# Both parts of the activations as one moving operand in the feature-major products of a two-block network

## The chip, the cores and the metric

One NeuronCore of one Trainium2 chip runs the whole kernel; inputs and outputs lie in the chip's memory. The metric is the device time of one execution in microseconds (us). Engines are named as in the profile: PE is TensorE's matmul, PEld its weight load, DVE is VectorE, ACT is ScalarE, POOL is GpSimd and SP is SyncE, which issues the DMAs of the weights.

## The reference

256 tokens of 2048 features (T = 256, D = 2048) go through two network blocks in float32. Nearly all arithmetic is products of the activations with weight matrices.

```python
def first_block(x, ...):                       # block 1
    h = rms_norm(x, norm1_w)
    proj = h @ w_in                            # 2048 x 10792
    q, kv, gates, dn_qkv, z, a, b, merge_g = split(proj)
    nsa = nsa_mixer(...) @ w_up_nsa            # attention, 1024 x 2048
    dn  = gated_deltanet(...) @ w_up_dn        # delta rule, 1024 x 2048
    x = x + (sigmoid(merge_g[0]) * nsa + sigmoid(merge_g[1]) * dn) @ w_o
    h = rms_norm(x, norm2_w)
    x = x + (silu(h @ w_ffn_gate) * (h @ w_ffn_up)) @ w_ffn_down   # 2048 x 5632, twice; 5632 x 2048
...
# block 2: RWKV-7 heads and latent attention (MLA) side by side, @ w_out, then
#   silu(causal_conv(h @ ffn_w_gate)) * (h @ ffn_w_up), @ ffn_w_down, closing norm
```

## The kernel before

A float32 matrix is written as a sum of two float32r parts, hi and lo. A product keeps three of the four part products: hi times hi, hi times lo, lo times hi (`mm3`, L288 to L292). Each weight tile is loaded raw (`wraw`, 512 KB), cast to hi by ACT (L259), and the rest is formed as lo by DVE (L260); the emission of the two is moved ahead of other work (`high_priority`). There are 5 raw, 3 hi and 3 lo buffers. `wchunks` (L265) loads 1024 // n rows of 128 at a time where a product is n < 512 columns wide, and two rows where n is 512.

Two kinds of product exist. Token-major (`gemm_tok`, L294): the activations are stationary and 512 weight columns move. Feature-major (`gemm_feat`, L304): a 128 x 128 block of the weights is stationary and the 256 tokens move; four blocks m = 0 to 3 (nm = 4; in `Rwkv.project` two) fill one tile `mmA` of PSUM, [128, 4, 256], over the kt = 16 (in `merge_up` 8) rows k of the weights. One block of one row is three matmuls of 256 columns. Of the pool `psA` there are two such tiles, two banks each; the other four banks are `pB`.

The two parts of the activations H lie in two 16 KB areas (slots b and c, or d and e; `hh` and `hl` in block 2's feed-forward). The results leave PSUM in one DVE or ACT operation of up to 1024 columns, mostly together with the multiplication by the norm's row scale (`rb`). Feature-major are: `Nsa.first` and `Nsa.q`, `DeltaNet.project` (its results wait in the list `raw`, at most two, for `conv`), `merge_gate`, `merge_up`, gate and up of both feed-forwards, and `Rwkv.project` (out by `padded`). By hand, and not through `gemm_feat`, are `Nsa.kv` (L1083), `Rwkv.small`, `small_proj` and `Mla.project` (L1716); the last has moving operands in two runs of 128 columns (L1739, L1740).

In the mixers of both blocks several chains of steps are emitted side by side by `weave`, which estimates when a step is ready; a product yields a filler step per row k. `K.later` holds the turning of a finished piece of x into H (`turn`: PE transposes, ACT makes hi, DVE lo); it is emitted after the fourth row of the next product.

Of the kernel before, what the change touches and what calls it, by code (L numbers as in the profile page):

```python
# [37 lines left out]
def make_consts():  # L38
    """shape-only tables: identity, triangular masks, block masks, rotary tables of the first block"""
# [82 lines left out]
class Traced:  # L122
    """an engine of nc whose calls are also counted"""
# [82 lines left out]

class Kern:
    def __init__(self, tc, A, out, ctx):
# [43 lines left out]
    def wsplit(self, raw, view, n):  # L252
        """raw tile [P, 1024], n elements used -> float32r (hi, lo) views with hi + lo == raw"""
# [11 lines left out]
    def wchunks(self, W, kt, c0, n, wk0=0, cols=None):  # L265
        """yields (k, hi, lo): the k-th 128 rows of W[:, c0:c0+n], or of the column ranges `cols`"""
# [21 lines left out]
    def mm3(self, o, a, b, start, stop):  # L288
        """o += (a0 + a1).T @ (b0 + b1) less the product of the two low parts"""
# [4 lines left out]
    def gemm_tok(self, X, W, kt, c0, n, xk0=0, wk0=0):  # L294
        """[tokens, n columns] in PSUM [P, 2, 512]; X = (hi, lo) [P, kt, T]; a step per 128 rows of W"""
# [8 lines left out]
    def gemm_feat(self, X, W, kt, c0, nm=4, xk0=0, wk0=0):  # L304
        """[128 columns, tokens] blocks in PSUM [P, 4, T]; a step per 128 rows of W"""
        ps = self.psA.tile([P, 4, T], F32, name="mmA")
        for k, wh, wl in self.wchunks(W, kt, c0, nm * P, wk0):
            for m in range(nm):
                ms = slice(m * P, (m + 1) * P)
                self.mm3(ps[:, m, :], (wh[:, ms], wl[:, ms]), [a[:, xk0 + k, :] for a in X],  # L310
                         k == 0 and m % 2 == 0, k == kt - 1)
            yield FILL
        return ps

    def split(self, src, hi, lo, scale=None):
        """hi + lo = src * scale in float32r parts"""
# [20 lines left out]
    def square(self, out, x, t):  # L337
        """out = sum of the squares of the rows of x, [P, up to 512]"""
# [19 lines left out]
    def row_scale(self, st, n=D, out=None):  # L358
        """1 / rms of the rows"""
# [6 lines left out]
    def spread(self, r):  # L366
        """the rows' scales [P, 2] along the free dimension of every partition"""
# [7 lines left out]
    def rows(self, x, r):  # L375
        """x [P, 2, n] times r"""
# [24 lines left out]
    def wake(self):  # L401
        """while nothing has arrived: the clock of TensorE goes up, ScalarE gets a table"""
# [25 lines left out]
        # blocks of 8: every partition (row of the inverse) gets all of its block  # L428
# [15 lines left out]
        # pairs of blocks of b: minus (odd block of X) (L between them) (even block of X); the odd rows are kept together  # L444
# [38 lines left out]
def run(gen):  # L483
    """emit all the steps of a generator; its value"""
# [7 lines left out]
def together(*gens):  # L492
    """steps of several generators in turn; (generator, steps at a time) or one step each"""
# [28 lines left out]
class Cat:  # L522
    """the blocks of two tiles in a row"""
# [11 lines left out]
def hT_tiles(K, slots):  # L535
    return tuple(K.slot(s, [P, KD, T], F32R) for s in slots)


def hidden(K, pool, slots):
    """the inner activations of a feed-forward layer, (hi, lo)"""  # L540
    return tuple(Cat(K.slot(s, [P, KD, T], F32R), pool.tile([P, KF - KD, T], F32R, name="hid" + n)) for s, n in zip(slots, "hl"))


def block1(K, ctx):
    """the first block; every norm's row scale is applied to what is made of the rows, so that no product waits for it"""
# [4 lines left out]
    H = hT_tiles(K, "bc")  # L550
# [3 lines left out]
    def begin():  # L554
        """x by column groups, between the weights of the first projection"""
# [17 lines left out]
    with ExitStack() as mix:  # L573
# [33 lines left out]
    H = hT_tiles(K, "de")  # L607
    run(add_proj(K, x, M, A["w_o"][0], KD, scale=0.5, after=norm_after(K, x, st, "norm2_w", H)))
    r = K.row_scale(st)
    with tc.tile_pool(name="ffn", bufs=1) as fp:  # L610
        hid = hidden(K, fp, "bc")
        for g in range(KF // 4):
            pg = run(K.gemm_feat(H, A["w_ffn_gate"][0], KD, 512 * g))
            if g == 0:
                rb = K.spread(r)
            sg = fp.tile([P, 4, T], F32, name="sg", bufs=2)
            rows4 = rb[:, None, :].to_broadcast([P, 4, T])
# [5 lines left out]
            K.split(sg, hid[0][:, 4 * g:4 * g + 4], hid[1][:, 4 * g:4 * g + 4])  # L623
        # x times the weight of the closing norm, with the sums for that norm and for the next
# [4 lines left out]
        H = hT_tiles(K, "de")  # L629
# [14 lines left out]
def norm_after(K, x, st, wname, H):  # L644
    """for add_proj: the pieces of x transposed and times the next norm's weight, and the sums of their squares"""
# [16 lines left out]
def add_proj(K, x, X, W, kt, scale=1.0, base=None, after=None, widths=(512,) * 4, **kw):  # L662
    """x += scale * (tokens of X) @ W, or x = x * base + that; `after` sees each piece"""
# [60 lines left out]
class DeltaNet:  # L724
# [1094 lines left out]
```

## Time and profile before

| | |
|---|---|
| time, median of 3 runs | 2887.51 us (2883.43 to 2891.77) |
| span of the profiled execution | 2890.4 us |
| PE busy | 2856.1 us, 99% of the span |
| DVE busy / ACT busy / POOL busy | 60% / 44% / 7% |
| weights and the rest read | 476.23 MB, 167 GB/s over the span |

The profiled execution has no other time than its span, from the first instruction to the last; it lies 2.9 us above the median and inside the range of the runs. In the rows, a PE matmul is listed with a duration longer than the distance from one to the next, since matmuls overlap in the array; distances are read from the starts, or from counts in a stretch in which PE is never idle.

### The profile page before, as it was taken

The numbers are of one execution on the slowest core, as the hardware profiler recorded it, in microseconds if no ns is written. First come the engines' busy times: TensorE is split into PE (matmuls) and PEld (weight loads), VectorE is DVE, ScalarE is ACT, GpSimd is POOL, SyncE is SP. The second block draws the span as 40 slices with busy tenths as digits, with TensorE's granted clock in tenths as the row PEclk, the third lists the DMA queues.
The fourth block names the chain that finished last, engine by engine and source line by source line (L and its number), as shares of the span: only waits on it lengthen the run. The fifth ranks groups of instructions, "written<-read, shape, count | busy, mean of one in ns | idle before, by whom it ended". The sixth has DMA issues, their size and how long they took to land.

```text
span 2890.4 us, 49301 instructions
## 1 busy us (share of the span) xinstructions
PE 2856.1 (99%) x20536; PEld 2654.7 (92%) x20536; DVE 1731.7 (60%) x2333; ACT 1270.6 (44%) x1568; POOL 204.3 (7%) x203
## 2 busy tenths in 40 slices
PE   9999999999999999999999999999999999999998
PEld 8997899999899999998888988888899999999888
DVE  6678557845555555554555685676575656655453
ACT  5447345434444444444444543444354444343443
POOL 0000000001000000000000221210000000000000
PEclk9999999999999999999999999999999999999999
DMA  7653256546666666666666652323466666666664
GB/s 233 205 153 106 84 167 178 162 129 189 215 182 184 183 181 188 182 183 188 198 196 195 189 146 74 99 73 115 142 172 190 183 182 183 183 183 189 193 193 139
DMA packets 285569, 484.68 MB, mean 168 GB/s; under 512 B 26113, under 2 KB 77057, under 8 KB 284706
## 3 DMA queue, kind: packets, MB, share of 16 engines
q1 hardware_dynamic: 282688, 475.88, 56.0%
q10 hardware_dynamic: 2658, 5.66, 0.6%
q8 instruction: 161, 2.64, 0.4%
q14 instruction: 62, 0.51, 0.0%
HBM read 476.23 MB, written 5.24 MB: 167 GB/s over the span
## 4 chain that ended last, share of the span: by engine, by line
PE 94%; DVE 3%; issue 1%; POOL 1%; ACT 1%; DMA 0%; ACTq 0%; DVEq 0%; POOLq 0%
PE mmA L134 83%; PE pB L134 11%; DVE wlo L260 1%; DVE MM L134 0%; DVE xn L134 0%; POOL psb L134 0%; DMA wA<-in_rwkv_w_dram 0%; DVE iw L134 0%; DVE sd L134 0%; DMA dn_nrm<-in_dn_norm_w_dram 0%; ACT whi L259 0%; POOL sa L134 0%; POOL xn L134 0%; DVE rt L134 0%; DVE Dm L134 0%
## 5 line engine op out<-in xcount | busy, mean ns | idle before, releaser
L260 DVE TENSOR_TENSOR wlo<-wraw,whi 128x1024 fp32r<-128x1024 f32 x889 | 1100.1, 1239 | 872.9 <-ACT whi L259 871.6
L259 ACT CAST whi<-wraw 128x1024 fp32r<-128x1024 f32 x889 | 928.2, 1045 | 1315.5 <-PE mmA L134 1250.3
L134 PE MATMUL mmA<-sd,whi 128*128 128x256 f32 x2256 | 604.7, 286 | 0.4 <-DVE xn L134 0.4
L134 PE MATMUL mmA<-sd,wlo 128*128 128x256 f32 x2048 | 582.2, 284 | 2.6 <-DVE wlo L260 2.6
L134 PE MATMUL mmA<-se,whi 128*128 128x256 f32 x2096 | 568.1, 284 | 1.2 <-DVE se L134 1.2
L134 PEld LDWEIGHTS mmA<-sd,whi 128*128 128x128 f32 x2256 | 420.6, 193 | 3.3 <-issue 1.6
L134 PE MATMUL mmA<-hh,whi 128*128 128x256 f32 x1408 | 398.7, 283 | 0.0
L134 PE MATMUL mmA<-hh,wlo 128*128 128x256 f32 x1408 | 398.5, 283 | 0.0
L134 PE MATMUL mmA<-hl,whi 128*128 128x256 f32 x1408 | 398.5, 283 | 0.0
L134 PEld LDWEIGHTS mmA<-sd,wlo 128*128 128x128 f32 x2048 | 394.6, 193 | 3.5 <-DVE wlo L260 3.0
L134 PEld LDWEIGHTS mmA<-se,whi 128*128 128x128 f32 x2096 | 393.1, 192 | 2.2 <-DVE se L134 1.4
L134 PE MATMUL mmA<-sb,whi 128*128 128x256 f32 x1152 | 332.7, 289 | 1.5 <-ACT whi L259 1.5
L134 PE MATMUL mmA<-sb,wlo 128*128 128x256 f32 x1152 | 329.3, 286 | 1.9 <-DVE wlo L260 1.9
L134 PE MATMUL mmA<-sc,whi 128*128 128x256 f32 x1152 | 328.8, 285 | 0.0
L134 PEld LDWEIGHTS mmA<-hl,whi 128*128 128x128 f32 x1408 | 270.3, 192 | 0.0
L134 PEld LDWEIGHTS mmA<-hh,whi 128*128 128x128 f32 x1408 | 270.3, 192 | 0.0
L134 PEld LDWEIGHTS mmA<-hh,wlo 128*128 128x128 f32 x1408 | 270.3, 192 | 0.0
L134 PEld LDWEIGHTS mmA<-sb,whi 128*128 128x128 f32 x1152 | 222.6, 193 | 3.9 <-ACT whi L259 1.7
L134 PEld LDWEIGHTS mmA<-sb,wlo 128*128 128x128 f32 x1152 | 222.7, 193 | 3.0 <-DVE wlo L260 2.3
L134 PEld LDWEIGHTS mmA<-sc,whi 128*128 128x128 f32 x1152 | 222.5, 193 | 1.4 <-issue 0.7
L134 PE MATMUL mmA<-whi,hidh 128*128 128x512 f32 (+1 forms) x504 | 184.2, 365 | 0.0
L134 PE MATMUL mmA<-wlo,hidh 128*128 128x512 f32 (+1 forms) x504 | 184.2, 365 | 0.0
(422 smaller groups left out, 3815.0 us busy)
## 6 DMA issues: line engine op xcount, KB each, us to landing
wraw<-in_w_in_dram SPq DMA_DIRECT2D x232, 512.0 KB, 3.7
wraw<-in_w_ffn_gate_dram SPq DMA_DIRECT2D x88, 512.0 KB, 3.9
wraw<-in_w_ffn_up_dram SPq DMA_DIRECT2D x88, 512.0 KB, 3.7
wraw<-in_w_ffn_down_dram SPq DMA_DIRECT2D x88, 512.0 KB, 4.5
wraw<-in_ffn_w_gate_dram SPq DMA_DIRECT2D x88, 512.0 KB, 3.8
wraw<-in_ffn_w_up_dram SPq DMA_DIRECT2D x88, 512.0 KB, 3.7
wraw<-in_ffn_w_down_dram SPq DMA_DIRECT2D x88, 512.0 KB, 3.7
wraw<-in_w_o_dram SPq DMA_DIRECT2D x32, 512.0 KB, 4.6
```

The lines of the kernel that those rows point to most:

```text
L134: r = f(out, *a, **k)
L259: nc.nc.scalar.copy(h, r)
L260: nc.nc.vector.tensor_sub(l, r, h.bitcast(F32))
```

## The change

`gemm_feat` computes two blocks (nm = 2) into the same PSUM tile, now [128, 2, 2, 256]. For each block the hi weights are stationary once and hi and lo of the activations move as one operand of 512 columns, in two runs of 256; then the lo weights are stationary and hi of the activations moves. So the first half of a block's bank holds hi·hi + lo·hi, the second half hi·lo. `fold` adds the halves: ACT copies the second half to SBUF, DVE adds the first half to it. H's two parts become one tile (`Parts`) so that one access covers both. Callers loop over groups of two blocks instead of four; the row scale is multiplied in SBUF after the fold; the list `raw` of the delta rule holds pairs of heads. The pool of the slots d and e is opened anew twice (`new_side`). `small_proj`, `Nsa.kv`, `Rwkv.small` and `Mla.project` stay as they are. The rest of the diff removes comments.

```diff
+class Parts:
+    def __init__(self, both):
+        self.both = both
+    def __getitem__(self, i):
+        return self.both[:, i]
+    def wide(self, k):
+        return self.both[:, :, k]
...
-    def gemm_feat(self, X, W, kt, c0, nm=4, xk0=0, wk0=0):
-        ps = self.psA.tile([P, 4, T], F32, name="mmA")
+    def gemm_feat(self, X, W, kt, c0, nm=2, xk0=0, wk0=0):
+        ps = self.psA.tile([P, 2, 2, T], F32, name="mmA")
         for k, wh, wl in self.wchunks(W, kt, c0, nm * P, wk0):
-            for m in range(nm):
-                ms = slice(m * P, (m + 1) * P)
-                self.mm3(ps[:, m, :], (wh[:, ms], wl[:, ms]), [a[:, xk0 + k, :] for a in X],
-                         k == 0 and m % 2 == 0, k == kt - 1)
+            self.wide(ps, X, xk0 + k, wh, wl, range(nm), k == 0, k == kt - 1)
             yield FILL
         return ps
+    def wide(self, ps, X, k, wh, wl, blocks, start, stop):
+        for m in blocks:
+            ms = slice(m * P, (m + 1) * P)
+            self.mm(ps[:, m], wh[:, ms], X.wide(k), start, stop)
+            self.mm(ps[:, m, 0], wl[:, ms], X[0][:, k], False, stop)
+    def fold(self, out, ps):
+        self.nc.scalar.copy(out, ps[:, :, 1])
+        self.nc.vector.tensor_tensor(out, ps[:, :, 0], out, op=ALU.add)
...
-        for g in range(KF // 4):
-            pg = run(K.gemm_feat(H, A["w_ffn_gate"][0], KD, 512 * g))
+        for g in range(KF // 2):
+            pg = run(K.gemm_feat(H, A["w_ffn_gate"][0], KD, 256 * g))
...
-            nc.vector.tensor_tensor(sg, pg, rows4, op=ALU.mult)
+            K.fold(sg, pg)
+            nc.vector.tensor_tensor(sg, sg, rows2, op=ALU.mult)
             nc.scalar.activation(sg, sg, AF.Silu)
-            nc.gpsimd.tensor_tensor(sg, sg, rows4, op=ALU.mult)
-            pu = run(K.gemm_feat(H, A["w_ffn_up"][0], KD, 512 * g))
-            nc.vector.tensor_tensor(sg, pu, sg, op=ALU.mult)
+            nc.gpsimd.tensor_tensor(sg, sg, rows2, op=ALU.mult)
+            pu = run(K.gemm_feat(H, A["w_ffn_up"][0], KD, 256 * g))
+            su = fp.tile([P, 2, T], F32, name="su", bufs=2)
+            K.fold(su, pu)
+            nc.vector.tensor_tensor(sg, su, sg, op=ALU.mult)
...
-    for g in range(4):
-        ps = yield from K.gemm_feat(X, W, 8, 512 * g)
-        gs = slice(4 * g, 4 * g + 4)
-        nc.vector.scalar_tensor_tensor(gate[:, gs], gate[:, gs], 1.0, ps, op0=ALU.add, op1=ALU.mult)
+    for g in range(8):
+        ps = yield from K.gemm_feat(X, W, 8, 256 * g)
+        gs = slice(2 * g, 2 * g + 2)
+        up = K.npool.tile([P, 512], F32, name="xn", bufs=3).rearrange("p (m t) -> p m t", m=2)
+        K.fold(up, ps)
+        nc.vector.scalar_tensor_tensor(gate[:, gs], gate[:, gs], 1.0, up, op0=ALU.add, op1=ALU.mult)
...
         for kind in (1, 0, 2):
-            while len(self.raw) > 1:
-                yield BLOCK
-            ps = yield from self.K.gemm_feat(self.H, self.w_in, KD, C_DN + 1024 * kind + 512 * grp)
-            self.raw.append(ps)
+            for hf in range(2):
+                while len(self.raw) > 1:
+                    yield BLOCK
+                ps = yield from self.K.gemm_feat(self.H, self.w_in, KD, C_DN + 1024 * kind + 512 * grp + 256 * hf)
+                self.raw.append(ps)
...
-            nc.vector.tensor_tensor(cb[:, :, 3:], ps[:, 2 * hf:2 * hf + 2], self.rb[:, None, :].to_broadcast([P, 2, T]), op=ALU.mult)
+            K.fold(cb[:, :, 3:], ps)
+            nc.vector.tensor_tensor(cb[:, :, 3:], cb[:, :, 3:], self.rb[:, None, :].to_broadcast([P, 2, T]), op=ALU.mult)
...
-            raw.append((kind, self.padded(pp, ps[:, 0:2])))
+            raw.append((kind, self.padded(pp, ps, K.fold)))
```

## Rows read from the trace of the kernel before

**Rows 1.** The page: span, busy time and instructions, and PE in 40 slices
```profile
span 2890.4 us, 49301 instructions
...
PE 2856.1 (99%) x20536; PEld 2654.7 (92%) x20536; DVE 1731.7 (60%) x2333; ACT 1270.6 (44%) x1568; POOL 204.3 (7%) x203
...
PE   9999999999999999999999999999999999999998
```
**Rows 2.** The page: chain that ended last, by engine
```profile
PE 94%; DVE 3%; issue 1%; POOL 1%; ACT 1%; DMA 0%; ACTq 0%; DVEq 0%; POOLq 0%
```
**Rows 3.** Windows: PE, PEld, DVE, ACT, POOL busy, clock, DMA share, GB/s
```profile
900.00:1000.00 100.00, 100.00 (x835) 100.00 (x834) 50.91 (x41) 40.92 (x39) 4.83 (x2) 1.00 0.65 185
2300.00:2400.00 100.00, 100.00 (x836) 100.00 (x835) 59.18 (x65) 40.90 (x40) 7.68 (x5) 1.00 0.65 183
2650.00:2750.00 100.00, 100.00 (x443) 82.79 (x442) 48.18 (x41) 40.48 (x41) 4.08 (x2) 1.00 0.61 194
```
**Rows 4.** Timeline of PE where narrow turns to wide, and wide to narrow
```profile
2634.91 0.28 PE L134 MATMUL mmA<-hh,wlo 128*128 128x256 f32 x1
2635.03 0.40 PE L134 MATMUL mmA<-whi,sa 128*128 128x512 f32 x1
2635.27 0.40 PE L134 MATMUL mmA<-wlo,sa 128*128 128x512 f32 x1
...
2814.35 0.39 PE L134 MATMUL mmA<-whi,hidl 128*128 128x512 f32 x1
2814.58 0.28 PE L134 MATMUL mmA<-whi,sa 128*128 128x256 f32 x1
2814.69 0.28 PE L134 MATMUL mmA<-wlo,sa 128*128 128x256 f32 x1
```
**Rows 5.** Groups by line: lo weights stationary, 256 columns moving (count, busy, mean ns)
```profile
L134 PE MATMUL mmA<-sd,wlo 128*128 128x256 f32 x2048 | 582.2, 284 | 2.6 <-DVE wlo L260 2.6
L134 PE MATMUL mmA<-sb,wlo 128*128 128x256 f32 x1152 | 329.3, 286 | 1.9 <-DVE wlo L260 1.9
L134 PE MATMUL mmA<-se,wlo 128*128 128x256 f32 x128 | 36.2, 283 | 0.0
```
**Rows 6.** Tile hh: its lo weights' matmuls, and hl's making (ns, first, last)
```profile
L134 PE MATMUL mmA<-hh,wlo x1408: 279/283/362, 2126.8 to 2634.9; 128*128 128x256 f32 x176
...
L134 DVE SCALAR_TENSOR_TENSOR hl<-pB,prm,hh x16: 471/474/483, 2120.5 to 2136.3; 128x256 fp32r<-128x256 f32 x16
```
**Rows 7.** Groups by line: evictions of PSUM and the splits of the weights
```profile
L134 ACT COPY psb<-mmA 128x512 f32<-128x512 f32 x13 | 7.6, 582 | 0.0
L134 DVE TENSOR_TENSOR cb<-mmA,rb 128x512 f32<-128x512 f32 x12 | 7.8, 686 | 3.4 <-PE mmA L134 3.4
L134 DVE TENSOR_TENSOR sg<-mmA,rb 128x1024 f32<-128x1024 f32 x11 | 13.5, 1224 | 7.0 <-PE mmA L134 7.0
L260 DVE TENSOR_TENSOR wlo<-wraw,whi 128x1024 fp32r<-128x1024 f32 x872 | 1083.9, 1245 | 864.0 <-ACT whi L259 862.8
L259 ACT CAST whi<-wraw 128x1024 fp32r<-128x1024 f32 x872 | 914.2, 1049 | 1290.6 <-PE mmA L134 1230.5 <-issue 44.0 <-ACT sg L134 9.1
```
**Rows 8.** Windows: the mixers of block 1 and block 2
```profile
224.00:370.00 146.00, 144.77 (x899) 117.15 (x898) 104.61 (x226) 77.66 (x138) 6.98 (x14) 0.95 0.33 93
...
470.00:660.00 190.00, 190.00 (x1483) 180.82 (x1482) 131.41 (x192) 84.87 (x100) 4.76 (x10) 1.00 0.52 153
...
1660.00:2070.00 410.00, 402.55 (x2757) 344.27 (x2755) 273.07 (x571) 180.13 (x299) 57.81 (x71) 0.97 0.34 102
```
**Rows 9.** Windows: two stretches whose weights come in runs of 1 KB
```profile
2817.00:2857.00 40.00, 40.00 (x336) 40.00 (x335) 19.68 (x21) 15.08 (x16) 5.79 (x4) 1.00 0.60 183
...
1600.00:1660.00 60.00, 58.70 (x469) 56.63 (x468) 39.94 (x45) 33.57 (x46) 20.89 (x24) 1.00 0.61 177
```
**Rows 10.** Timeline of PE in MLA: matmuls whose moving operand lies in two runs
```profile
1965.53 0.28 PE L134 MATMUL mmA<-whi,sd 128*128 128x256 f32 x1
1965.65 0.28 PE L134 MATMUL mmA<-wlo,sd 128*128 128x256 f32 x1
```

More of the change, by code (lines that the diff above doesn't have):

```diff
@@ L218, in __init__, with pair, new_side @@
         self.cst = None
+        self.sides = ctx.enter_context(ExitStack())
+        self.new_side()
         self.later = []
     def slot(self, which, shape, dt=F32):
-        return (self.h2 if which in "bc" else self.hpool).tile(shape, dt, name="s" + which, tag="slot_" + which)
+        return (self.hpool if which == "a" else self.side).tile(shape, dt, name="s" + which, tag="slot_" + which)
+    def pair(self, which):
+        return Parts((self.h2 if which == "bc" else self.side).tile([P, 2, KD, T], F32R, name="s" + which, tag="slot_" + which))
+    def new_side(self):
+        self.sides.close()
+        self.side = self.sides.enter_context(self.tc.tile_pool(name="side", bufs=1, side="right"))
     def load_head(self):
@@ L532, in __getitem__, with hidden @@
         return tile_[(p, slice(s.start - o, s.stop - o) if isinstance(k, slice) else k - o, *c)]
[L535 to L541, printed above, removed]
+def hidden(K, pool, heads):
+    return tuple(Cat(h, pool.tile([P, KF - KD, T], F32R, name="hid" + n)) for h, n in zip(heads, "hl"))
 def block1(K, ctx):
@@ L549, in block1 @@
     K.wake()
-    H = hT_tiles(K, "bc")
+    H = K.pair("bc")
     st = K.sums()
@@ L600, in block1 @@
         weave(K, dn.chunks(0), dn.chunks(1), dn.ready(1), fill())
-        M = hT_tiles(K, "bc")
+        M = K.pair("bc")
         run(merge_up(K, dn.odn, A["w_up_dn"][0], td[0], tn, M))
+    K.new_side()
     x = K.slot("a", [P, 2, D])
@@ L606, in block1 @@
     st = K.sums()
-    H = hT_tiles(K, "de")
+    H = K.pair("de")
     run(add_proj(K, x, M, A["w_o"][0], KD, scale=0.5, after=norm_after(K, x, st, "norm2_w", H)))
@@ L628, in block1 @@
         st = K.sums()
-        H = hT_tiles(K, "de")
+        H = K.pair("de")
         def after(g, t, xg):
@@ L678, in merge_gate @@
 def merge_gate(K, H, w_in, rb, half, dst):
-    for g in range(4):
-        ps = yield from K.gemm_feat(H, w_in, KD, C_MG + 2048 * half + 512 * g)
-        d = dst[:, 4 * g:4 * g + 4]
-        K.nc.vector.tensor_tensor(d, ps, rb[:, None, :].to_broadcast([P, 4, T]), op=ALU.mult)
+    for g in range(8):
+        ps = yield from K.gemm_feat(H, w_in, KD, C_MG + 2048 * half + 256 * g)
+        d = dst[:, 2 * g:2 * g + 2]
+        K.fold(d, ps)
+        K.nc.vector.tensor_tensor(d, d, rb[:, None, :].to_broadcast([P, 2, T]), op=ALU.mult)
         K.nc.scalar.activation(d, d, AF.Tanh, scale=0.5)
@@ L991, in first @@
         K, nc = self.K, self.K.nc
+        raw = K.npool.tile([P, 512], F32, name="xn", bufs=3).rearrange("p (m t) -> p m t", m=2)
         ps = yield from K.gemm_feat(self.H, self.w_in, KD, C_KV)
+        K.fold(raw, ps)
+        ps = yield from K.gemm_feat(self.H, self.w_in, KD, C_KV + 256)
+        K.fold(self.raw[1], ps)
         K.load_mix(op, "sin")
@@ L1083, in q @@
     def q(self, hk):
-        ps = yield from self.K.gemm_feat(self.H, self.w_in, KD, C_Q + 512 * hk)
-        rope(self.K, self.pool, ps, 4, self.qT[:, 4 * hk:4 * hk + 4])
+        for h in range(4 * hk, 4 * hk + 4, 2):
+            ps = yield from self.K.gemm_feat(self.H, self.w_in, KD, C_Q + P * h)
+            q = self.K.npool.tile([P, 512], F32, name="xn", bufs=3).rearrange("p (m t) -> p m t", m=2)
+            self.K.fold(q, ps)
+            rope(self.K, self.pool, q, 2, self.qT[:, h:h + 2])
     def streams(self):
@@ L1250, in fill @@
                     yield BLOCK
+            K.new_side()
             M.load(R.cos2, R.sin2)
@@ L1276, in block2 @@
     with tc.tile_pool(name="ffn2", bufs=1) as fp:
-        H = [fp.tile([P, KD, T], F32R, name="h" + n) for n in "hl"]
+        H = Parts(fp.tile([P, 2, KD, T], F32R, name="hh"))
         run(add_proj(K, x, R.y, w_out, 2, xk0=6, wk0=6, after=norm_after(K, x, sm, "ffn_norm_g_2", H)))
         r = K.row_scale(sm)
-        hid = hidden(K, fp, "ae")
-        for g in range(KF // 4):
-            pg = run(K.gemm_feat(H, A["ffn_w_gate_2"][0], KD, 512 * g))
+        hid = hidden(K, fp, [K.slot(s, [P, KD, T], F32R) for s in "ae"])
+        for g in range(KF // 2):
+            pg = run(K.gemm_feat(H, A["ffn_w_gate_2"][0], KD, 256 * g))
             if g == 0:
                 rb = K.spread(r)
-            rows4 = rb[:, None, :].to_broadcast([P, 4, T])
-            cb = fp.tile([P, 4, T + 2], F32, name="cb")
-            sg = fp.tile([P, 4, T], F32, name="sg")
+            gs = slice(2 * g, 2 * g + 2)
+            rows2 = rb[:, None, :].to_broadcast([P, 2, T])
+            cb = fp.tile([P, 2, T + 2], F32, name="cb", bufs=2)
+            sg = fp.tile([P, 2, T], F32, name="sg", bufs=2)
             nc.gpsimd.memset(cb[:, :, 0:2], 0.0)
-            nc.vector.tensor_tensor(cb[:, :, 2:], pg, rows4, op=ALU.mult)
-            for m in range(4):
-                ct = 4 * g + m
+            K.fold(cb[:, :, 2:], pg)
+            nc.vector.tensor_tensor(cb[:, :, 2:], cb[:, :, 2:], rows2, op=ALU.mult)
+            for m in range(2):
+                ct = 2 * g + m
                 w = [K.p("ffn_conv_w_2", KF * i + ct) for i in range(3)]
@@ L1296, in block2 @@
             nc.scalar.activation(sg, sg, AF.Silu)
-            nc.gpsimd.tensor_tensor(sg, sg, rows4, op=ALU.mult)
-            pu = run(K.gemm_feat(H, A["ffn_w_up_2"][0], KD, 512 * g))
-            nc.vector.tensor_tensor(sg, pu, sg, op=ALU.mult)
-            K.split(sg, hid[0][:, 4 * g:4 * g + 4], hid[1][:, 4 * g:4 * g + 4])
+            nc.gpsimd.tensor_tensor(sg, sg, rows2, op=ALU.mult)
+            pu = run(K.gemm_feat(H, A["ffn_w_up_2"][0], KD, 256 * g))
+            su = K.npool.tile([P, 512], F32, name="xn", bufs=3).rearrange("p (m t) -> p m t", m=2)
+            K.fold(su, pu)
+            nc.vector.tensor_tensor(sg, su, sg, op=ALU.mult)
+            K.split(sg, hid[0][:, gs], hid[1][:, gs])
         wb = row_weights(K, fp, A["final_norm_g_2"])
@@ L1423, in small @@
         self.rb = K.spread(self.r)
-        pt = [self.padded(pp, ps[:, 2 * i:2 * i + n]) for i, n in ((0, 2), (1, 1))]
+        pt = [self.padded(pp, ps[:, 2 * i:2 * i + n], nc.scalar.copy) for i, n in ((0, 2), (1, 1))]
         self.sh = bp.tile([P, 3, T], F32, name="sh")
```

34 lines of the change are left out of this document (16 added, 18 removed).

## The prediction

> **What bounds the kernel now.** I read the page first: PE is busy 99% of the span and in every one of the 40 slices [rows 1], and the chain that ended last is PE for 94% [rows 2]. Busy time alone could hide a slow PE, so the second view is the windows: in the feed-forwards PE runs at full clock, never idle, with 835 or 836 narrow matmuls (256 columns) in 100 us, and with 443 wide ones (512 columns) in a token-major product [rows 3]. That gives 100 / 835.5 = 119.7 ns for a narrow matmul and 100 / 443 = 225.7 ns for a wide one. So 256 more columns cost 106.0 ns, about a column a cycle at 2.4 GHz, and each matmul costs 119.7 - 106.0 = 13.7 ns beside its columns, whatever its width. That fixed part is what the change can save. DVE at 51 to 59% and ACT at 41% in these windows wait for PE, not PE for them: the cast of the weights' hi part stood idle for 1230.5 us until PE gave a buffer back [rows 3, 7].
>
> **The change: the blocks.** A block of one weight row is three narrow matmuls now, 3 x 119.7 = 359.1 ns, and becomes a wide and a narrow one: 225.7 + 119.7 = 345.4 ns. Saved: 13.7 ns. The narrow matmul with lo weights occurs once in each block, so its rows count the blocks: 2048 + 1152 + 128 [rows 5] + 1408 [rows 6] = 4736. The products made by hand keep theirs: `Nsa.kv` 2 x 16 x 2 = 64, `Rwkv.small` 3 x 16 = 48, `Mla.project` 48 + 32 = 80, together 192. There remain 4544: 2816 in the two feed-forwards, 1344 in block 1's mixer, 384 in `Rwkv.project`. 4544 x 13.7 = 62.3 us: 38.6, 18.4 and 5.3.
>
> The trace of before has no stream in which wide and narrow alternate, only single changes. A wide one after a narrow one stands 0.24 us ahead of the next, a narrow one after a wide one 0.11 us [rows 4], against 0.23 and 0.12 in uniform streams: sum 0.35 either way, so the sum of the uniform prices holds. The bounds are the two mixed sums, 0.34 and 0.36 us: a gain of 19 ns (86 us in all) or a loss of 1 ns (4 us). The new wide operand lies in two runs; MLA's narrow matmuls with two runs stand 0.12 us apart like all others [rows 10], so I charge nothing for it.
>
> One rule of the skill speaks against the gain. The Trainium skill, "TensorE: Matmul & The Clock Gate", section "Back-to-back issue gap", gives a warm gap of N / 2.4 + 2.5 ns, which puts the fixed part at 2.5 ns; a block would then save 2.5 ns, 11 us in all, by an estimate from that page. The rows above, 119.7 and 225.7 ns, differ from the page's 109 and 216, and the measurement decides.
>
> **The fold.** 150 products (88 in the feed-forwards, 2 and 4 in `first` and `q`, 12 in the delta rule, 16 + 16 in the merges, 12 in RWKV) each get an ACT copy of 512 columns, 582 ns, and a DVE add, 686 ns by the like operation with one PSUM operand [rows 7]. RWKV's 12 copies exist already: ACT + 138 x 0.58 = 80 us, DVE + 150 x 0.69 = 103 us. A DVE operation of 1024 cut into two of 512 costs 2 x 686 - 1224 = 148 ns more, some 90 times: 13 us. DVE goes from 1731.7 to about 1850 us, 65%, and in the second feed-forward from 59 to about 67%. All this lies beside PE if two conditions hold. First, PSUM: with two tiles a fold must end before the following product does, 16 x 2 x 345 ns = 11.1 us later (23 us before), in `merge_up` 8 x 2 x 345 = 5.5 us. A fold is 1.27 us; behind a cast on ACT (1.05) and a split and one eviction on DVE (1.25 + 0.69) it is 4.3 us, so it is hidden in both. Without that cover it costs 150 x 1.27 = 190 us. Second, the weights: the copy is a new wait of ACT on PE's last matmul, and behind it stand the casts, behind the add the splits, and PE waits for those. A chunk of 512 KB is 8 blocks, 2.76 us, and three buffers put the split two chunks, 5.5 us, ahead of its use; cast and split need 1.05 + 1.25, which leaves 3.2 us, against 1.27 for the fold and 0.69 for the multiplication behind it. Before, the longer evictions of 1.22 us and a whole convolution stood there, and PE was never idle [rows 3]. Price 0.
>
> **The weights' DMAs.** 256 columns instead of 512 mean runs of 1 KB instead of 2 KB, four rows in a DMA instead of two; number and bytes of the DMAs stay. Needed is 524288 B / 2.76 us = 190 GB/s (182 before). The last product of the kernel already loads runs of 1 KB: 183 GB/s at a DMA share of 0.60 with PE never idle, no dearer per byte than 2 KB at 0.65 and 183 to 185 [rows 9, 3]. Price 0.
>
> **The mixers and the seams.** In RWKV PE is idle 7.5 of 410 us and the clock averages 0.97 [rows 8], so part of the work hangs on chains; the 12 folds add 12 x 0.69 = 8.3 us to chains, if all of it counts, nothing if none does. I take 5, which cancels the stage's saving. In the delta rule `raw` now holds two pairs of heads, not two groups of four: PE's stock of filler falls from 46 to 22 us. The stage from 224 to 370 us has PE idle 1.2 us and a clock of 0.95 [rows 8]; I take 2 us, between 0 and the 7 us that half the clock cost there (5% of 146). At both feed-forwards the last four rows of H are turned while the first product runs: its last `hl` starts 9.5 us after the product's first matmul [rows 6], 3.7 us after the turn's place (4 rows of 1.44 us, 5.8 us in). Row 12 is now due 8 x 2 x 0.345 = 5.5 us after that place, not 11.5: hidden, but barely; 0 to 2 us each, I take 1 each. The `q`, `first` and `new_side` edits move nothing that PE waits for; I take 0. The start stays bound by PE and x arrives earlier, since only one chunk of weights stands between its pieces.
>
> **Sum.** 62.3 - 5 - 2 - 2 = 53 us off 2890.4 gives 2837; against the median, 2887.5 - 53 = 2834.5 us, which I forecast as 2835.
>
> **The rivals.**
> (a) The mixers are bound by chains, and PE's savings there become idle time: only the feed-forwards gain, 38.6 less 2: 2851. For it: PE idle and half clock in rows 8. Against: from 470 to 660 us, where delta rule and merges run together, PE has no idle time [rows 8].
> (b) Alternation costs 0.34 us a block: 86 - 9 = 77 us, 2810. For: the lower of the changes in rows 4. Against: the two changes balance.
> (c) The fixed part is not saved, because it goes with runs or columns: block 359 ns, the charges stay: 2887.5 + 9 = 2896. Against: wide matmuls carry it once, two runs cost nothing [rows 3, 10].
> By the page's 2.5 ns instead it would be 2887.5 - 11 + 9 = 2885, which belongs to this case.
> (d) Slower, by runs of 1 KB: if they can't pass 177 GB/s, as measured while RWKV's weights came in [rows 9], a chunk takes 524288 / 177 = 2.96 us in place of 2.87, and 4544 / 8 = 568 chunks cost 51 us: 2938. It decides below 182 GB/s. Against: 183 GB/s at a share of 0.60.
> (e) Slower, by the fold: PE waits for a PSUM tile in each product, + 190 - 62: 3015. It decides where a fold ends over 11.1 us (5.5 in `merge_up`) after its product. In `merge_up` alone it is 16 x 1.27 = 20 us and stays inside the range.
>
> **How the numbers follow.** Forecast 0.65, with 2822 to 2848 of its own; (a) 0.15, (b) 0.05, (c) 0.07, (d) 0.04, (e) 0.04. The range 2815 to 2858 holds the forecast and (a) and leaves 0.20 out. A measurement of this kernel tells 0.3%, 8.7 us, from no change: faster are the forecast, (a) and (b), 0.85; within it most of (c), 0.06; slower (d), (e) and the rest of (c), 0.09.
>
> **What would show it.** In a feed-forward window of 100 us PE stays at 100 with about 579 matmuls (2 per 345 ns), half of them 128x512; the wide and the narrow starts stand 0.23 and 0.11 to 0.12 us apart. PE's count falls by 4544 to about 15990. DVE shows 65%. The DMA share is about 0.62 at 190 GB/s. Gate and up of the second feed-forward end 19 us earlier after their start. It is wrong if idle time of PE in these windows ends on `wlo`, `whi`, `sg` or `cb`, if a pair of starts is not 0.345 us, or if the mixers lose more than 20 us together.

## The result and the profile after

The changed kernel takes 2859.07 us (median of 4 runs, 2856.85 to 2862.17) against 2887.20 us of the kernel before: ratio 0.9905, 95% interval 0.9889 to 0.9921. The gain is 28 us, not the 53 forecast; 2859 lies 1 us above the range.

The page of the kernel after (span, busy time, PE in 40 slices, the chain that ended last), against [rows 1, 2]:

```profile
span 2859.1 us, 40723 instructions
...
PE 2825.8 (99%) x15992; PEld 2414.1 (84%) x15992; DVE 1840.9 (64%) x2575; ACT 1338.7 (47%) x1762; POOL 219.5 (8%) x242
...
PE   9999999999999999999999999999999999999998
...
PE 94%; DVE 3%; issue 1%; POOL 0%; DMA 0%; ACT 0%; ACTq 0%; DVEq 0%; SPq 0%; POOLq 0%
```

PE has 4544 matmuls fewer, as counted, and it is as busy as before. So nothing new is waited for in the large; the matmuls that are left must take longer than the sum said. The windows of the kernel after (PE, PEld, DVE, ACT, POOL busy, clock, DMA share, GB/s), in the order of [rows 3, 8]: two in the feed-forwards, one in a token-major product, three in the mixers:

```profile
900.00:1000.00 100.00, 100.00 (x572) 87.64 (x571) 57.44 (x58) 46.98 (x54) 9.03 (x5) 1.00 0.61 187
2300.00:2400.00 100.00, 100.00 (x568) 86.73 (x567) 69.59 (x88) 46.01 (x54) 7.01 (x10) 1.00 0.60 188
2620.00:2720.00 100.00, 100.00 (x440) 82.57 (x439) 47.63 (x41) 40.41 (x41) 4.08 (x2) 1.00 0.58 192
224.00:370.00 146.00, 145.90 (x832) 114.75 (x831) 106.38 (x213) 76.93 (x126) 7.96 (x15) 1.00 0.41 115
470.00:660.00 190.00, 188.81 (x1122) 161.83 (x1121) 133.31 (x199) 90.54 (x113) 8.31 (x8) 1.00 0.54 158
1624.00:2034.00 410.00, 400.32 (x2463) 330.39 (x2462) 272.33 (x573) 173.44 (x294) 57.67 (x72) 0.94 0.31 94
```

In the feed-forwards PE is never idle at full clock, but only 572 and 568 matmuls lie in 100 us, not 579. In block 1's mixer the clock is 1.00 where it was 0.95, in block 2's it is 0.94 where it was 0.97 (1 is 2.4 GHz; half clock is 1.2 GHz). The stages of the two profiled runs, cut at the first issue of the weights that follow (us):

| stage | before | after | gain | forecast |
|---|---|---|---|---|
| block 1's mixer, to the issue of `w_o` | 716.5 | 691.4 | 25.1 | 16.4 |
| `w_o` | 87.2 | 88.7 | -1.5 | 0 |
| gate and up, first feed-forward | 508.6 | 495.8 | 12.8 | 18.3 |
| down, up to block 2's constants | 266.5 | 266.9 | -0.4 | 0 |
| block 2's mixer, to gate of the second | 527.9 | 542.8 | -14.9 | 0 |
| gate and up, second feed-forward | 510.8 | 501.3 | 9.5 | 18.3 |
| down and the end | 272.9 | 272.2 | 0.7 | 0 |

The profiled run of the kernel before has a mean clock of 0.990, as low as any of the 28 runs listed further down (0.990 to 0.996), so what the table owes to half clock in block 1's mixer belongs to this pair of executions.

Two questions follow: why a block (one wide, one narrow matmul) is dearer than 345.4 ns, and why block 2's mixer lost 15 us. The timeline of PE in the second feed-forward, the kernel after (start, duration, operation):

```profile
2299.66 0.40 PE L134 MATMUL mmA<-hh,whi 128*128 128x512 f32 x1
2299.90 0.28 PE L134 MATMUL mmA<-hh,wlo 128*128 128x256 f32 x1
2300.01 0.40 PE L134 MATMUL mmA<-hh,whi 128*128 128x512 f32 x1
2300.26 0.28 PE L134 MATMUL mmA<-hh,wlo 128*128 128x256 f32 x1
2300.38 0.40 PE L134 MATMUL mmA<-hh,whi 128*128 128x512 f32 x1
2300.61 0.28 PE L134 MATMUL mmA<-hh,wlo 128*128 128x256 f32 x1
2300.72 0.40 PE L134 MATMUL mmA<-hh,whi 128*128 128x512 f32 x1
```

Three blocks last 2300.72 - 2299.66 = 1.06 us. To the ns the distances repeat: 240, 120, 236, 114, 232, 118, sum 1060, so 353.3 ns a block; in the first feed-forward 234, 120, 234, 120, 224, 122 or nearly so, and the mean is 351.1 ns a block. Read the same way, uniform narrow matmuls of the kernel before stand 120.0 ns apart and uniform wide ones 226.7: a block before is 360.0 ns, and the uniform sum is 346.7.

### The profile page after: what moved, and what is told of

Its sections match the earlier page's. It is cut to its first block, busy times and chain, and to the rows that moved or that the text cites. A ratio compares the mean times of both kernels' runs of the same rounds, so it can differ in the third digit from the quotient of the medians.

```text
span 2859.1 us, 40723 instructions
## 1 busy us (share of the span) xinstructions
PE 2825.8 (99%) x15992; PEld 2414.1 (84%) x15992; DVE 1840.9 (64%) x2575; ACT 1338.7 (47%) x1762; POOL 219.5 (8%) x242
## 4 chain that ended last, share of the span: by engine, by line
PE 94%; DVE 3%; issue 1%; POOL 0%; DMA 0%; ACT 0%; ACTq 0%; DVEq 0%; SPq 0%; POOLq 0%
PE mmA L134 83%; PE pB L134 11%; DVE wlo L285 1%; DVE xn L134 0%; DVE iw L134 0%; DMA cst<-in_consts_dram 0%; DVE sd L134 0%; ACT whi L284 0%; DVE MM L134 0%; DMA dn_nrm<-in_dn_norm_w_dram 0%; POOL sa L134 0%; DVE tmp L134 0%; POOL psb L134 0%; DVE hh L134 0%; DVE Dm L134 0%
## 5 line engine op out<-in xcount | busy, mean ns | idle before, releaser
L134 PE MATMUL mmA<-sde,whi 128*128 128x512 f32 (+1 forms) x1888 | 655.0, 391 | 5.5 <-DVE iw L134 3.2
L134 PE MATMUL mmA<-sde,wlo 128*128 128x256 f32 x1840 | 523.6, 285 | 1.7 <-DVE wlo L285 1.7
L134 PE MATMUL mmA<-hh,whi 128*128 128x512 f32 x1408 | 497.7, 399 | 0.0
L134 PEld LDWEIGHTS mmA<-sde,whi 128*128 128x128 f32 x1888 | 353.2, 189 | 84.2 <-issue 3.9
L134 PE MATMUL mmA<-sbc,whi 128*128 128x512 f32 (+1 forms) x1216 | 413.9, 388 | 1.7 <-DVE sbc L134 1.7
L134 PEld LDWEIGHTS mmA<-sde,wlo 128*128 128x128 f32 x1840 | 347.7, 189 | 3.7 <-DVE wlo L285 2.2
L134 PE MATMUL mmA<-sbc,wlo 128*128 128x256 f32 x1152 | 325.5, 283 | 1.8 <-DVE wlo L285 1.8
L134 PEld LDWEIGHTS mmA<-sbc,whi 128*128 128x128 f32 x1216 | 224.7, 189 | 50.7 <-ACT whi L284 1.9
L134 PE MATMUL mmA<-whi,sbc 128*128 128x512 f32 (+1 forms) x768 | 231.1, 375 | 0.0
L134 PEld LDWEIGHTS mmA<-sbc,wlo 128*128 128x128 f32 x1152 | 218.4, 190 | 3.8 <-DVE wlo L285 2.2
```

The costliest lines, as they stand in the source:

```text
L134: r = f(out, *a, **k)
```

## The experiments

The blocks' prices below are the mean distance from start to start in the two feed-forwards (850 to 1200 us and 2150 to 2500 us). "Theory 1" and the like are named in the expectations, which were written before each run.

**Two runs, or the alternation?** `contig`: the parts of H lie side by side, so the wide operand is one run of 512 columns.

```diff
-tile([P, 2, KD, T], F32R, ...)   wide(k): self.both[:, :, k]
+tile([P, KD, 2, T], F32R, ...)   wide(k): self.both[:, k]
```

> Changed against the kernel after: the two parts of H lie side by side for each row k, [128, 16, 2, 256], so the wide moving operand is one contiguous run of 512 columns and not two runs of 256 that stand 16 KB apart; the same for the operands of the two merges. Numbers and order of all instructions stay. Theory 1 (the two runs make the wide matmul dearer, 231 to 236 ns in the feed-forwards against 225.7): wide starts 0.226 us ahead of the next, a block 345 to 347 ns, 4544 x 6 to 8 ns = 27 to 36 us less, about 2828 us. Theory 2 (alternation of wide and narrow costs, whatever the addresses): a block stays at 351 to 354 ns, time 2859 us within 0.3%. Theory 3 (it is where in SBUF the operand lies against the weights that are being loaded): the two feed-forwards change by different amounts, either way, 2845 to 2870 us.

Measured: 2858.99 us; blocks 351.1 and 353.3 ns, as after. Theory 1 falls: two runs cost nothing.

`pairs`: the order within a row k is wide, wide, narrow, narrow.

```diff
         for m, ms in cols:
             self.mm(ps[:, m], wh[:, ms], X.wide(k), start, stop)
+        for m, ms in cols:
             self.mm(ps[:, m, 0], wl[:, ms], X[0][:, k], False, stop)
```

> Changed against the kernel after: for each row k the order wide 0, narrow 0, wide 1, narrow 1 becomes wide 0, wide 1, narrow 0, narrow 1; same matmuls, half as many changes of width. Theory 2 (the change of width costs 6 to 8 ns a block): the cost halves, 4544 x 3 to 4 ns = 14 to 18 us less, about 2843 us, two blocks in 696 to 700 ns instead of 702 to 707. Theory 1 (two runs): two blocks stay at 702 to 707 ns, time 2859 us within 0.3%.

Measured: 2840.04 us; blocks 348.3 ns in both feed-forwards. Window of the kernel pairs:

```profile
2300.00:2400.00 100.00, 100.00 (x576) 87.32 (x575) 70.05 (x88) 46.21 (x55) 5.79 (x10) 1.00 0.62 189
```

576 where after has 568: the order of the same matmuls is worth 5 ns a block there and 3 in the first feed-forward, as theory 2 expected.

`narrow`: all of the change, but the wide matmul cut into two narrow ones.

```diff
-            self.mm(ps[:, m], wh[:, ms], X.wide(k), start, stop)
+            self.mm(ps[:, m, 0], wh[:, ms], X[0][:, k], start, False)
+            self.mm(ps[:, m, 1], wh[:, ms], X[1][:, k], False, stop)
```

> Changed against the kernel after: the wide matmul is cut back into two of 256 columns (hi and lo of the activations one after the other with the same hi weights), so a block is three narrow matmuls as in the kernel before; folds, groups of two blocks, runs of 1 KB and the new layout all stay. It prices all of the change but the wide matmul. If folds, DMAs and seams are hidden and RWKV alone pays: a block of 359 ns, so 4544 x 6 to 8 ns = 27 to 36 us over the kernel after, about 2890 us, RWKV and MLA together some 15 us longer than in the kernel before. If the rest of the change costs nothing at all: 2887 us less 0 to 3. If it costs the 25 us that the forecast was out by: 2912 us.

Measured: 2897.60 us, ratio 1.0061 (1.0044 to 1.0079). Windows of the kernel narrow, two feed-forwards and block 2's mixer:

```profile
1649.00:2059.00 410.00, 399.43 (x2692) 341.62 (x2691) 274.48 (x577) 175.46 (x297) 57.73 (x74) 0.95 0.32 94
900.00:1000.00 100.00, 100.00 (x835) 100.00 (x835) 56.37 (x57) 45.17 (x52) 7.17 (x4) 1.00 0.59 182
2300.00:2400.00 100.00, 100.00 (x836) 100.00 (x835) 66.85 (x85) 45.03 (x53) 6.64 (x8) 1.00 0.60 184
```

835 and 836 matmuls in 100 us, as in [rows 3]: folds, smaller groups and runs of 1 KB hide wholly. But block 2's mixer is 539.3 us long although its matmuls are those of before (527.9): the wide matmul is not needed for its loss. And block 1's mixer is 704.1 us long against 716.5 before, with no half clock between 20 and 700 us: of the 25.1 us that after gained there, 12.4 come without any change of width, and 704.1 - 691.4 = 12.7 with it.

`allwide`: the lo weights move the wide operand too (lo times lo is computed in addition).

```diff
-            self.mm(ps[:, m, 0], wl[:, ms], X[0][:, k], False, stop)
+            self.mm(ps[:, m], wl[:, ms], X.wide(k), False, stop)
```

> Changed against the kernel after: the lo weights too move the wide operand, so each block is two wide matmuls in two runs and no width ever changes in a feature-major product (it computes lo times lo in addition, which nobody asked for). Theory 1 (two runs cost 6 to 8 ns in each wide one): a block of 2 x 233 = 466 ns, 4544 x 114 = 518 us over the kernel after, 3377 us. Theory 2 (only the change of width costs): a block of 2 x 225.7 = 451 ns, 4544 x 99 = 450 us more, 3309 us; 443 wide matmuls in 100 us of the feed-forwards against 429 by theory 1.

Measured: 3321.53 us (one run), nearer to theory 2. Window of the kernel allwide in the second feed-forward:

```profile
2600.00:2700.00 100.00, 100.00 (x443) 82.88 (x442) 52.34 (x64) 36.46 (x42) 4.21 (x6) 1.00 0.47 147
```

443 feature-major wide matmuls, as many as token-major ones in [rows 3]: 226.7 ns apart, in two runs, without a change of width. In the first feed-forward, with H in the slots d and e, they stood 232 ns apart. That was not expected, and `hpright` and `pad` follow it.

**How the width change costs.** `eights`: in the feed-forwards eight wide matmuls, then eight narrow ones (four rows k of a chunk); the mixers as in pairs.

```diff
+        for k, m, ms, wh, wl in todo:      # four rows, two blocks
+            self.mm(ps[:, m], wh[:, ms], X.wide(xk0 + k), ...)
+        for k, m, ms, wh, wl in todo:
+            self.mm(ps[:, m, 0], wl[:, ms], X[0][:, xk0 + k], ...)
```

> Changed against the kernel of the run pairs: in the two feed-forwards the four rows k of a weight chunk are taken together, eight wide matmuls and then eight narrow ones, so the width changes twice in 16 matmuls instead of twice in 4; the mixers keep the order of pairs. If it is the change of width that costs in the second feed-forward (block 353.4 ns alternating, 348.3 in pairs, uniform prices 226.7 + 120.0 = 346.7): 347 to 348 ns there, 1408 x 1 = 1 to 2 us under pairs. In the first feed-forward, where a uniform stream of wide matmuls whose operand lies in the slots d and e took 232 ns each: if that place costs by itself, the block comes out at 232 + 120 = 352 ns, 5 us over pairs; if it does not, 347 to 348 as in the second. Time 2836 to 2846 us, against 2840 of pairs.

Measured: 2854.20 us, 8 us over the range expected; blocks 351.2 and 349.2 ns (means over whole groups of 16 matmuls). In the second feed-forward the distances after each change are the same in nearly every group: wide 233, 236, 228, 233, 231, then 227, 227, 227; narrow 113, 119, then six times 120. So a change to wide makes five wide matmuls dearer, together by 1160.7 - 5 x 226.7 = 27 ns, and the change to narrow gives 7 ns back: 20 ns for both. Spread over eight blocks that is the 349.2 measured (346.7 + 20 / 8), but in pairs, with both changes in two blocks, it would be 346.7 + 20 / 2 = 356.7, and pairs has 348.3. The first feed-forward, 351.2, speaks for a second cost by place. Of the 14 us over pairs 3 remain when the clock is taken out (last table).

`swap`: alternation stays, but the narrow matmul adds to the other block's bank of PSUM (in short form, by block).

```diff
-hi(0), lo(0), hi(1), lo(1)
+hi(0), lo(1), hi(1), lo(0)
```

> Changed against the kernel after: wide and narrow matmuls still alternate, but the narrow one goes to the other block's bank of PSUM: wide 0, narrow 1, wide 1, narrow 0 for each row k but the first. If a block is 351 to 354 ns because a narrow matmul adds to the half of a bank that the wide one just before it is still writing (in pairs, 348.3 ns, no narrow one follows a wide one of its own bank): the block falls to 346 to 348 ns in the second feed-forward, 4544 x 4 to 6 ns = 18 to 27 us less, about 2835 us. If it is the change of width as such: 353 ns stay, 2857 us within 0.3%.

Measured: 2856.77 us; blocks 351.1 and 353.3 ns, as after. The bank is not the cause.

`fours`: as pairs_rwkv_pad (below), with four wide and four narrow matmuls in the feed-forwards (one of four such lines).

```diff
-K.gemm_feat(H, A["w_ffn_gate"][0], KD, 256 * g)
+K.gemm_feat(H, A["w_ffn_gate"][0], KD, 256 * g, rows=2)
```

> Changed against the kernel of the run pairs_rwkv_pad: in the two feed-forwards two rows k are taken together, four wide matmuls and then four narrow ones; the mixers keep pairs. A block is 353.3 ns where wide and narrow alternate (1 and 1), 348.3 with 2 and 2, 350.0 with 8 and 8 (second feed-forward), 346.7 by the sum of the uniform streams. If the cost goes with the number of changes and eight are dearer for another reason: 347 to 348 ns, 1408 blocks of each feed-forward x 0.8 = 2 us under pairs_rwkv_pad, 2825. If it is the run of wide matmuls itself that is dear when only hi weights are stationary one after the other: 348.5 to 350 ns, 2828 to 2832 us.

Measured: 2843.52 us; blocks 350.8 ns in both feed-forwards, above even the second expectation (whose 350.0 for eights is 349.2 by whole groups). One, two, four and eight of a width cost 353.3, 348.3, 350.8 and 349.2 ns (second feed-forward): not a price for each change. That the order of the widths sets the price is shown, since the matmuls are the same; what in the engine makes it so stays open.

**Places in SBUF.** `hpright`: slot a at the upper end, d and e 16 KB lower. `pad`: 384 bytes set aside at the upper end. No instruction changes.

```diff
-self.hpool = ctx.enter_context(tc.tile_pool(name="hpool", bufs=1))
+self.hpool = ctx.enter_context(tc.tile_pool(name="hpool", bufs=1, side="right"))    # hpright
+ctx.enter_context(tc.tile_pool(name="pad", bufs=1, side="right")).tile([P, 96], F32, name="pad")    # pad
```

> Changed against the kernel after: only places in SBUF. Slot a, 16 KB, is opened at the upper end, so the pool of the slots d and e moves down by 16 KB (from 196576 to 229344 to 180192 to 212960), slot a comes to lie at 212960 to 229344 (it was at 64096), and everything on the left side above it moves down by 16 KB too. If the upper end costs (wide matmuls from the slots d and e took 232 ns in a uniform stream, those from other places 226.7; token-major ones with the stationary slot e 232 to 234 instead of 226 to 227): the first feed-forward's wide matmul falls from 230.6 by some 4 to 6 ns, 1408 x 5 = 7 us less, and those with slot a stationary rise by 6; together 2850 to 2854 us. If places do not matter: the same starts as after in both feed-forwards, 2859 us within 0.3%.

> Changed against the kernel after: 384 bytes are set aside at the upper end of SBUF, so the slots d and e begin at 196192 and 212576 and not at 196576 and 212960; no instruction changes. Theory 4 (it is the start of an operand against a boundary that costs: 196576 is 480 more than a multiple of 512, all places whose uniform wide stream took 226 to 227 ns are 96 more than one, as 196192 is): the token-major wide matmuls with slot e stationary fall from 232 to 234 ns to 226 to 227, and the first feed-forward's block from 351 ns to that of the second, 353, or under it, 347, if alternation costs only there by the place; time 2848 to 2862 us. Rival (it is the upper end of SBUF itself): 232 to 234 ns stay, and the 351 ns too.

Measured: 2857.35 us and 2860.13 us. In hpright both feed-forwards keep their patterns, and wide matmuls with slot a stationary go from 227 to 232 ns; those with slot e stay at 232 or above. Slot e is 16 KB lower there, so it is not the upper end itself. In pad they fall. Timeline of PE, the kernel after, in the last product, rows whose stationary operands are slots a and e:

```profile
2605.63 0.39 PE L134 MATMUL mmA<-whi,sa 128*128 128x512 f32 x1
2605.86 0.39 PE L134 MATMUL mmA<-wlo,sa 128*128 128x512 f32 x1
2606.09 0.40 PE L134 MATMUL mmA<-whi,se 128*128 128x512 f32 x1
2606.33 0.39 PE L134 MATMUL mmA<-whi,sa 128*128 128x512 f32 x1
```

and the kernel pad:

```profile
2608.20 0.39 PE L134 MATMUL mmA<-whi,sa 128*128 128x512 f32 x1
2608.42 0.39 PE L134 MATMUL mmA<-wlo,sa 128*128 128x512 f32 x1
2608.65 0.39 PE L134 MATMUL mmA<-whi,se 128*128 128x512 f32 x1
2608.88 0.39 PE L134 MATMUL mmA<-whi,sa 128*128 128x512 f32 x1
```

Three of them take 0.70 us after and 0.68 in pad; over all such rows the means are 227.0 + 232.4 + 234.1 and 226.8 + 226.7 + 227.1 ns. By the addresses on record with `hpright` and `pad` (no trace lists them) slot e begins 480 bytes above a multiple of 512 in after (and slot a in hpright), 96 above one in pad, like every place that never cost. So theory 4 holds for uniform streams, as far as two remainders can show it; which boundary counts, 512 bytes or another, is not shown. It fails for the block: with the better place the first feed-forward takes the second's pattern, 353.3 ns instead of 351.1, which costs 3 us and takes back the 2 us won. So the first feed-forward's 351.1 was a matter of place, and 353.3 is what strict alternation costs at a place that costs nothing by itself.

**Block 2's mixer.** `rwkv_old`: RWKV's products alone go back to three narrow matmuls and one ACT copy.

```diff
-            ps = yield from K.gemm_feat(self.H, self.w_in, KD, 1024 * kind + 256 * q, nm=2)
-            raw.append((kind, self.padded(pp, ps, K.fold)))
+            ... mm3 per block, as before ...
+            raw.append((kind, self.padded(pp, ps[:, 0:2], K.nc.scalar.copy)))
```

> Changed against the kernel after: the products of RWKV alone go back to three narrow matmuls a block, and their 12 results leave PSUM by one ACT copy each without a fold; all else stays as after. If the fold and the new product in RWKV are what lengthens block 2's mixer (568.6 us from the loading of its constants to the second feed-forward's first weights, against 553.7 before, with 48 us at half clock against 24): the stage goes back to 554 to 558 us and the half clock to 24, so 2859 - 12 = 2847 us. If it is only where the steps of the chains come to lie, whatever moved them: the stage stays within 560 to 575 us, the 384 blocks cost 7 ns more each, 2.7 us, and the time is 2859 to 2865 us.

Measured: 2841.20 us, ratio 0.9846 (0.9816 to 0.9876): the median lies 18 us under that of after, by using the change less. The stage lasts 526.9 us. Its window in the kernel rwkv_old:

```profile
1624.00:2034.00 410.00, 402.36 (x2759) 343.00 (x2758) 273.99 (x574) 179.97 (x298) 57.53 (x70) 0.98 0.33 103
```

Clock 0.98 against 0.94 after. The profiled runs had half clock in this stage for 20.5 us (rwkv_old), 23.9 (before), 51.2 (after) and 41.0 (narrow). Where it begins in after, the timeline of PE:

```profile
1677.68 1.03 PE L134 MATMUL pB<-wA,hw 65*128 65x256 f32 x4
1681.94 0.47 PE L134 MATMUL mmA<-sde,whi 128*128 128x512 f32 x1 [3.24 <-DVE iw L134]
...
1682.96 0.33 PE L134 MATMUL mmA<-sde,wlo 128*128 128x256 f32 x1
1683.09 0.63 PE L134 MATMUL mmA<-sde,whi 128*128 128x512 f32 x1
```

and of DVE, the same kernel:

```profile
1678.79 2.35 DVE L285 TENSOR_TENSOR wlo<-wraw,whi 128x1024 fp32r<-128x1024 f32 x2
1681.05 0.74 DVE L134 TENSOR_SCALAR xn<-mmA,rl 128x512 f32<-128x512 f32 x1
1681.71 0.23 DVE L134 TENSOR_TENSOR iw<-pB,iw 128x8 f32<-128x8 f32 x2
```

PE stands still for 3.24 us. The profile names `iw`, which ended just then; the matmul writes an `mmA` tile, and I read the wait as one for DVE, behind two splits of weights, to empty that tile (`xn`, ended 1681.79). The same wait in pairs is put down to `xn`, and PE starts 0.14 us after it there, 0.15 here. 1 us later the clock falls and a wide matmul's record grows from 0.40 to 0.63 us. In rwkv_old the splits and the emptying come in another order, and PE has no idle time from 1670 to 1690 us.

But this stretch of half clock lasts only 3.4 us. The others in after are 17.1 us (from 1717.2), 3.4 (1864.0), 23.9 (1891.3) and 3.4 (1993.7); rwkv_old, whose stage starts at the same 1542.9 us, has 13.7 (1713.0), 3.4 (1866.6) and 3.4 (1893.9). So most of the difference begins at 1891 us, where PE had waited for another result of DVE, `bt`. Timeline of PE in after, then the same window in after and in rwkv_old:

```profile
1889.80 0.41 PE L134 MATMUL pB<-ident,bt 128*128 128x128 f32 x2 [1.49 <-DVE bt L134]
```

```profile
1889.00:1917.00 28.00, 26.58 (x134) 23.43 (x134) 10.16 (x27) 7.98 (x14) 1.04 (x3) 0.57 0.05 16
1889.00:1917.00 28.00, 26.07 (x184) 22.71 (x183) 22.43 (x60) 15.13 (x27) 2.10 (x4) 0.94 0.23 66
```

rwkv_old waits there too, 1.21 us at 1891.7, and has 3.4 us of half clock behind it, not 23.9. No single wait explains the stretches: pairs waits 1.89 us at 1674.8 and its clock stays up, and ahead of the stretch at 1717.2 PE has no wait of over 0.25 us for 35 us. With the fold in RWKV this stage lasted 538.9 to 542.8 us in seven of eight profiled runs (allwide, with more work, left out) and 528.7 in that of pairs; without it 524.7 to 528.2 in five (before among them). That RWKV's fold, with the steps that come with it, costs the kernel after time, and through the clock, is shown: the four runs of after have a mean clock of 0.988 to 0.991, those of rwkv_old 0.994 to 0.998, and narrow, with the fold and without the width, has 0.988 to 0.991. For the order of pairs it is not shown: there the stage was short with the fold. That the fold acts through the order of DVE's work is argued from these rows; no run changed that order alone.

`pairs_rwkv` joins the edits of pairs and rwkv_old, `pairs_rwkv_pad` adds that of pad.

> Two changes together against the kernel after: the order wide, wide, narrow, narrow of the run pairs and RWKV's old products of the run rwkv_old. If both causes stand side by side: a block of 348.3 ns in the feed-forwards and no more than 24 us of half clock in block 2's mixer, 2841 - (4160 blocks x 4 ns) = 2841 - 17 = 2824 us. If the half clock falls where it likes, whatever RWKV's products are: 2824 to 2845 us.

> As pairs_rwkv, with the 384 bytes set aside at the upper end of SBUF as in the run pad. By theory 4 the first feed-forward's block comes out at 347 to 348 ns and 160 rows of token-major matmuls lose 13 ns each, 2 us: 2820 to 2823 us. By its rival, nothing: as pairs_rwkv within 2 us.

Measured: 2837.44 us and 2827.49 us, ratio 0.9814 (0.9785 to 0.9842). The first is 13 us over "both causes side by side" and inside the range of its rival, that the half clock falls where it likes: pairs had the short stage already in its profiled run, so the second edit had little left to win there, and it gives RWKV's own block savings back; by the table below it changes the loss to the clock by 1 us. The second is 4 us over the range of theory 4: the first feed-forward's block is 348.3 ns with and without the pad, not 347 to 348, and only the token-major rows gain. The profiled spans, 2835.2 and 2833.4, differ by the 2 us expected of the pad; the rest of the 10 us between the medians is the clock, a mean of 0.993 to 0.994 in all runs of the one and 0.997 in three of four of the other. The page of pairs_rwkv_pad, the fastest kernel here:

```profile
span 2833.4 us, 41475 instructions
...
PE 2799.1 (99%) x16376; PEld 2412.7 (85%) x16376; DVE 1825.7 (64%) x2563; ACT 1340.0 (47%) x1762; POOL 219.9 (8%) x242
```

**The two causes apart.** Every run lists its mean granted clock. The kernel before was run 28 times beside these experiments, 2875.84 us at 0.996 to 2892.48 at 0.990; time x clock is 2863.5 to 2865.8 in all of them, so its whole spread is clock. The product is worked out, not measured, and good to some 1.5 us by the last digit of the clock (for the others the mean over their runs). It assumes that all work slows with the clock; the 28 runs bear that out.

| kernel | median, us | time x clock | lost to the clock |
|---|---|---|---|
| before (28 runs) | 2876 to 2892 (median 2882) | 2865 | 11 to 28 |
| narrow | 2898 | 2865 | 32 |
| after | 2859 | 2830 | 29 |
| contig, swap, hpright, pad | 2857 to 2860 | 2828 to 2831 | 27 to 31 |
| rwkv_old | 2841 | 2831 | 11 |
| pairs | 2840 | 2820 | 20 |
| eights | 2854 | 2823 | 31 |
| fours | 2844 | 2824 | 19 |
| pairs_rwkv | 2837 | 2819 | 19 |
| pairs_rwkv_pad | 2827 | 2819 | 9 |

At full clock the change gains 35 us, all of it by the wide matmul (narrow gains none). Against the 2887.2 us of its own comparison, which by the same product lost 22 to the clock, after loses 29: 35 - 7 = 28 us, what was measured. Against the median of the 28 runs it would be 23 us: how much clock the kernel before happens to lose is in the number.

## Why the prediction was wrong

- **The block: the step that failed.** A pair was to cost 345.4 ns by the uniform prices, with 0.34 and 0.36 us as bounds. It costs 351.1 and 353.3 in the feed-forwards. The mechanism is right (one fixed part less for each block: allwide, 226.7 ns), but the sum of uniform prices doesn't hold for an alternating stream. The bounds were sound and held the truth; the middle was taken because two single changes balanced to 10 ns, where one block's whole saving is 13.7, and the dear end was left to rival (c) with a chance of 0.07. The gate and up products gained 8.9 x 1408 = 12.5 and 6.7 x 1408 = 9.4 us, not 19.3 each: 17 of the missing 25 us, and the second feed-forward's gate and up end 9.5 us earlier, not 19. The 1728 other blocks, at about 350 ns (the mean of the pairs in block 1's mixer, 347 to 352 by stretch), save 17, not 23.7: 6 more.
- **A small error on the way.** 100 / 835.5 = 119.7 is a count of records that touch the window; a record of 0.28 us touches both edges, and the starts give 120.0 and 226.7. The fixed part is 13.3 ns, not 13.7: 2 us of 62, held in the above.
- **RWKV: a step put at nothing.** Zero was forecast, a saving of 5.3 against 5 for folds on the chains. At full clock that is nearly so: 2830 with the change in RWKV, 2831 without it. But the stage got 27 us more of half clock (51.2 against 23.9), and 15 us longer in the profiled pair. Half clock stood in [rows 8] and was priced only for block 1's mixer.
- **Block 1's mixer** gained 25 us against 16.4: its 20.5 us of half clock (161 to 168 and 345 to 359 us) are gone, about 10 us. The forecast named the opposite sign, 2 us. This part is luck: the profiled run of before was one at the lowest clock.
- **The sum as it came out.** At full clock 62 - 23 for the dearer blocks is 39, and 35 were measured, so all the charges together were some 4 us, not 9. The clock took 7 more: 28.
- **Right:** fold and weights' DMAs at nothing (narrow; 187 and 188 GB/s at a share of 0.61 and 0.60, forecast 190 at 0.62), DVE at 64% (65), PE's count 15992 (15990), no cost for two runs (contig), starts 0.22 to 0.24 and 0.11 to 0.12 us apart. Rivals (a), (d) and (e) did not happen, nor (b); of (c) half did, for another reason than runs or columns.
- **A rule of a page.** The Trainium skill, "TensorE: Matmul & The Clock Gate", section "Back-to-back issue gap", would have saved 2.5 ns a block, 11 us, by an estimate from its formula for an isolated matmul. The measured 6.7 to 11.7 ns (360.0 less 353.3, 348.3) lie between that and the forecast; uniform streams here stand at 120.0 and 226.7 ns, not at the formula's 109 and 216, so the trace does not agree with it.

## What to carry to other kernels

A price from a uniform stream is not the price in a mixed one: where a change makes a new sequence of instructions, take the dear end of the bounds as a case of its own. Group matmuls of one width (wide, wide, narrow, narrow gave 3 to 5 ns a block for nothing) and try the order, since more grouping was not better. Where PE is not full, price a new step also by what it may do to the clock. Multiply each run's time by its granted clock before two kernels are compared. Put a change first where PE is always full.

## What was not expected of the hardware

- Alternating 512- and 256-column matmuls settled into a pattern of three blocks (1060 ns) instead of the sum of the uniform prices (1040); after a change from 256 to 512 columns five matmuls were dearer (233, 236, 228, 233, 231 ns) before 226.7 returned.
- Where an operand starts mattered to TensorE: 480 bytes above a multiple of 512 a uniform wide stream took 232 ns a matmul, 96 above one 226.7, and 384 bytes of padding decided it. Only these two places were tried. In the alternating stream the "worse" place was 2 ns a block better.
- The spread of the kernel before, 17 us, is all granted clock: 28 runs of 2876 to 2892 us give 2863.5 to 2865.8 us when multiplied by it.
- Half clock is not a matter of one wait of PE: 1.49 us of waiting was followed by 23.9 us of it, 1.21 us at the same place by 3.4, and 1.89 us elsewhere by none.
